# Layer 0 of a hybrid decoder: attention scores by pairs of heads, another column order in the finest decay level, query copies on GpSimd

## The chip, the cores and the metric

The kernel runs on one core of one Trainium2 chip. Its time is the device time of one execution in microseconds (us). A core has TensorE (PE in the profile, its weight loads PEld), VectorE (DVE), ScalarE (ACT), GpSimd (POOL) and SyncE (SP, which here issues every DMA). Each engine works through a queue of its own in order, and semaphores tie the queues together.

## The reference

The input is 256 tokens of width 1024. Layer 0 norms them, multiplies by one wide input matrix, and runs two mixers side by side: softmax attention (8 heads of width 64, causal, and with 256 tokens a single block, so that no block is chosen) and gated linear attention (GLA, 8 heads, keys 32 wide, values 64 wide), whose decay differs by token and key channel:

```python
b = jnp.cumsum(gi, axis=2)
diff = b[:, :, :, None, :] - b[:, :, None, :, :]
decay = jnp.exp(jnp.where(causal[:, :, None], diff, -jnp.inf))
attn = jnp.einsum('bhtd,bhsd,bhtsd->bhts', qi, ki, decay)
o = (jnp.einsum('bhts,bhsv->bhtv', attn, vi)
     + jnp.einsum('bhtd,bhdv->bhtv', qi * jnp.exp(b), state))
```

Both outputs are joined, projected back and added to the tokens. Then follow a gated convolutional feed-forward net (up to 2 x 3072, down from 3072), layer 1 (a recurrent block whose decay needs softplus(-lambda), a constant per channel), a second feed-forward net and a last norm. All of it is float32.

## The kernel before, in words

**Weights.** The large weights are cut into 204 chunks of 128 x 1024 floats (`w`). `load_w()` hands them out in order; `issue_w()` starts a chunk's DMA on SP, has ACT round it to `wh` (line 134) and DVE take the rest `wl = w - wh` (line 135). Every large product is three fast passes, `wh` with both parts of the activations and `wl` with the high part (`passes`, line 146): 24 matmuls of 256 columns for each chunk. The tiles that these products fill name the stages: `psbq`, `psbk` (GLA's q, k), `psa` (the attention's q, k), `pst` (both values), `psog` (output gate), `psout` (output projection), `psu` and `psd` (feed-forward up and down).

**Order.** The program is written in data-flow order; a scheduler places every instruction in its engine's queue and chooses memory. Only `order(a, b)` and the hooks bind it: `norm.rstd(hook=n)` makes the rounding of chunk n on ACT stand behind the norm's square root, that chunk's subtraction on DVE behind the reciprocal, and chunk n+1's rounding behind the copy of the result `rs`. Here n is 4.

**The start of layer 0.** `psg` gives the gate's low-rank product, `nps` the sum of squares and, transposed, the inverse root `rs`; `psz`, `z`, `az`, `G`, three scans (`cum`) and exponentials (`E`, `KR`) give the decays at widths 64, 16 and 4. `qn` is GLA's scaled query. `q0` is four copies of it, one for each head of a group of four, at the partitions of that head (32 rows each) with zeros elsewhere; ACT makes them (line 393), eight copies of 32 x 256. DVE multiplies `q0` by `E` into `qb`.

**GLA's scores** (`gla_attn`). Blocks of tokens are split into four levels. Levels 0 to 2 use `qb` and write runs of 64, 16 or 4 columns. The finest level uses `q0` itself: its product for offset I takes column I of every four, for the queries that it reads and for the PSUM that it writes (`pl<-q,kb`). There are 16 such products, each four heads x 32 columns. `copy_predicated` then moves what the masks `mu` allow into `at`.

**Softmax attention** (`softmax`). Head by head: scores of the first 128 queries, then the causal mask added by a bf16 product of the identity with `caus`, scores of the other 128 queries against 256 keys, mask again; DVE takes the maximum, ACT the exponentials, DVE scales, PE transposes (`ptr`) and multiplies with the values (`pso`). Even heads lie at partitions 0 to 63, odd heads at 64 to 127. Two banks (`pss`) serve in turn.

**Constants.** 23 tiny DVE instructions on 128 x 8 (lines 371 to 382, tiles `s`) make layer 1's constant `cc`; the casts of masks and identity (`mu`, `caus`, `identb`) are DVE's too. A bank is 2 KB per partition of PSUM.

Of the kernel before, what the change touches and what calls it, by code (L numbers as in the profile page):

```python
# [22 lines left out]
P = 128  # L23
S = 256
# [38 lines left out]
def trunk(ctx: ExitStack, tc: tile.TileContext, xT, w, wgk, wgk2, vec, cst, mskf, out):  # L63
# [22 lines left out]
    def V(name, i):  # L86
        o = VOFF[name] + i
        return vt[:, o:o + 1]
# [119 lines left out]
        return hi  # L208

    def residual(ps, m, X, gname, gi, norm):  # L210
        nc.vector.tensor_add(h[:, m, :], h[:, m, :], ps)  # L211
        norm.add(h[:, m, :])
        if X is not None:
            scaled_split(X, m, h[:, m, :], V(gname, gi * KT + m))

    def out_proj(M):
        acc = [bank(f"psout{i}", "g" if i < 3 else "l") for i in range(4)]
# [60 lines left out]
    with tc.tile_pool(name="l0", bufs=1) as lp, tc.tile_pool(name="l0r", bufs=4) as lr:  # L278
# [17 lines left out]
        mu = lp.tile([P, 3 * P], U8, name="mu")  # L296
        for i, n in enumerate(MSK):
            msk[n] = mu[:, i * P:(i + 1) * P]
        caus = lp.tile([P, P], BF16, name="causb")
        identb = lp.tile([P, P], BF16, name="identb")  # L300

        LV = [(1, 64, 1), (4, 16, 1), (16, 4, 1), (64, 1, 0)]
# [10 lines left out]
        q0 = [lp.tile([P, 4, S], F32, name=f"q0_{i}") for i in range(2)]  # L313
        for hf in range(2):
            nc.gpsimd.memset(q0[hf], 0.0)
        qns = {}
        at0 = [lp.tile([P, 4, S], F32, name=f"at0_{i}") for i in range(2)]
        at1 = [lp.tile([P, 4, P], F32, name=f"at1_{i}") for i in range(2)]
# [10 lines left out]
                             skip_group_check=True)  # L329
        for _ in range(4):  # L330
            nc.tensor.matmul(pw, wz[:, 0:P], wz, start=True, stop=True)
        rs = norm.rstd(hook=4)
        rtok = norm.tok
        bgk = lp.tile([32, S], F32, name="bgk")
        nc.vector.tensor_mul(bgk, psg[0:32, :S], rs[0:32, :])
        nc.sync.dma_start(ct, cst[:, P:])
        nc.sync.dma_start(mf, mskf)
        nc.vector.tensor_copy(mu, mf)
        nc.vector.tensor_copy(caus, C("caus"))
        nc.vector.tensor_copy(identb, idt)  # L340
# [30 lines left out]
        nc.vector.tensor_scalar(d2, e, 2.0, None, op0=ALU.add)
        nc.vector.reciprocal(d2, d2)
        nc.vector.tensor_mul(zz, e, d2)
        nc.vector.tensor_mul(z2, zz, zz)
        nc.vector.tensor_scalar(acc, z2, 1.0 / 17, 1.0 / 15, op0=ALU.mult, op1=ALU.add)
        for n in (13, 11, 9, 7, 5, 3, 1):
            nc.vector.tensor_mul(acc, acc, z2)
            nc.vector.tensor_scalar(acc, acc, 1.0 / n, None, op0=ALU.add)
        nc.vector.tensor_mul(acc, acc, zz)
        nc.vector.tensor_scalar(d2, lam, -1.0, 0.0, op0=ALU.mult, op1=ALU.max)  # L380
        nc.vector.scalar_tensor_tensor(acc, acc, 2.0, d2, op0=ALU.mult, op1=ALU.add)
        nc.vector.tensor_scalar(cc, acc, -8.0, None, op0=ALU.mult)
# [5 lines left out]
        for hf in range(2):  # L388
            qn = qns[hf] = lp.tile([P, S], F32, name=f"qn{hf}")
            nc.vector.scalar_tensor_tensor(qn, ps[:, hf * S:(hf + 1) * S], 32 ** -0.5, rs, op0=ALU.mult, op1=ALU.mult)  # L390
            for g in range(4):
                r = slice(32 * g, 32 * g + 32)
                nc.scalar.activation(q0[hf][r, g, :], qn[r, :], AF.Copy)
# [18 lines left out]
        def gla_prep(hf):  # L412
            hs = slice(hf * S, (hf + 1) * S)
            for li, (npar, wdt, i0) in enumerate(LV):
                def v4(ap):
                    return ap.rearrange("p (a j b) -> p a j b", j=4, b=wdt)
                kv, rv, ev = v4(kn[:, hs]), v4(KR[wdt][:, hs]), v4(E[wdt][:, hs])
                for I in range(i0, 4):
                    kb = v4(Kb[li, I])
                    J = I - i0  # L420
                    if i0:
                        nc.vector.tensor_mul(kb[:, :, J, :], kv[:, :, J, :], rv[:, :, J, :])
                    else:
# [12 lines left out]
            for li, wdt in enumerate((64, 16, 4)):  # L436
                Qb.append(lr.tile([P, 4, S], F32, tag="qb", bufs=4, name="qb"))
                nc.vector.tensor_mul(Qb[li], q0[hf], E[wdt][:, None, hs].to_broadcast([P, 4, S]))
            return Qb + [q0[hf]]

        def gla_attn(hf, qs):
            pa, pb = bank("pa", "l"), bank("pb", "l")
# [10 lines left out]
            for i in range(2):  # L453
                ts_ = slice(i * P, (i + 1) * P)
                dst = a0[:, :, 0:P] if i == 0 else a1
                for li, mn in ((1, "m64"), (2, "m16"), (3, "m4")):
                    npar, wdt, i0 = LV[li]
                    ps = bank("pl", "l")
                    def v5(ap):
                        return ap.rearrange("p g (a c) -> p g a c", c=4 * wdt)  # L460
                    pv = v5(ps.rearrange("p (g t) -> p g t", g=4))
                    qv = v5(qs[li][:, :, ts_])
                    for I in range(i0, 4):
                        cs = slice(I * wdt, (I + 1) * wdt)
                        nc.tensor.matmul(pv[:, :, :, cs], Kb[li, I][:, ts_], qv[:, :, :, cs], start=True, stop=True)  # L465
# [39 lines left out]

        PT = {}

        def softmax(hd):
            m, r = hd // 2, slice(64 * (hd % 2), 64 * (hd % 2) + 64)
            q, k = rot["q", m // 2][:, m % 2, :], rot["k", m // 2][:, m % 2, :]  # L510
            ps = bank("pss", "s")
            nc.tensor.matmul(ps[:, 0:128], q[r, 0:P], k[r, 0:P], start=True, stop=False)
            nc.tensor.matmul(ps[:, 0:128], identb, caus, start=False, stop=True)
            nc.tensor.matmul(ps[:, 128:384], q[r, P:S], k[r, 0:S], start=True, stop=False)  # L514
            nc.tensor.matmul(ps[:, 256:384], identb, caus, start=False, stop=True)
            mx = lr.tile([P, 2], F32, tag="mx", name="mx")
            nc.vector.tensor_reduce(mx[:, 0:1], ps[:, 0:128], axis=mybir.AxisListType.X, op=ALU.max)
            nc.vector.tensor_reduce(mx[:, 1:2], ps[:, 128:384], axis=mybir.AxisListType.X, op=ALU.max)
# [15 lines left out]
        av = lp.tile([P, 2, 512], F32, tag="v", name="av")  # L534
        tok_gemm(av)
        for pr in range(4):
            for j in range(2):
                PT[2 * pr + j] = softmax(2 * pr + j)
            ps = bank("pso", "t")
            for j in range(2):  # L540
                hd = 2 * pr + j
                r = slice(64 * j, 64 * j + 64)
                cs = slice(64 * hd, 64 * hd + 64)
                nc.tensor.matmul(ps[r, 0:S], av[:, 0, cs], PT[hd][:, 0:S], start=True, stop=False)
                nc.tensor.matmul(ps[r, P:S], av[:, 1, cs], PT[hd][:, S:384], start=False, stop=True)
            split(M[:, pr, 0, :], M[:, pr, 1, :], ps[:, :S])
# [53 lines left out]
        for n in range(4):  # L600
            tail(n, fin)

    def ffn(layer, X, norm, nextg):
        rs = norm.rstd()
        with tc.tile_pool(name=f"f{layer}", bufs=1) as yp, tc.tile_pool(name=f"f{layer}r", bufs=3) as fr:
# [225 lines left out]
```

## Time and profile before

| | |
|---|---|
| three timed runs | 645.31, 649.29, 649.80 us; median 649.29 |
| the profiled execution | 646.74 us; its span, first to last instruction, 645.0 us |
| busy time in the span | PE 630.7, DVE 513.3, ACT 406.0, POOL 8.9 us |
| TensorE's granted clock | 0.993 on the mean |
| read from memory | 109.01 MB, 171 GB/s |

A profile row gives the line, the engine, the operation, output and input tiles, the shape, how often, and then busy time and mean duration, or in a timeline start and length. Matmuls overlap, so a row's length holds the pipeline's depth too: what a group of matmuls costs is the distance from its start to the start of what follows.

### The profile page before, as it was taken

Reading aid. Unit: us, or ns where it says so; the run is one execution under the profiler, and the core shown is the slowest. Engines: PE = TensorE matmul, PEld = TensorE weight load, DVE = VectorE, ACT = ScalarE, POOL = GpSimd, SP = SyncE. Lnnn points to the kernel's source line nnn. Section 1 sums busy time; section 2 is a strip of 40 time slices with the busy share of each in tenths; the row PEclk is TensorE's granted clock in tenths of the full one; section 3 lists DMA queues with packets and bytes.
Section 4 is the critical chain, followed back from the end, with each engine's and each line's share of the span. In section 5 each row is a group of like instructions: output and inputs, shape, how many; then the busy total and the mean of one; then the engine's idle time right before and its main releaser. Section 6 shows DMA issues by size and latency. Waiting matters only on the chain.

```text
span 645.0 us, 12988 instructions
## 1 busy us (share of the span) xinstructions
PE 630.7 (98%) x5218; PEld 613.1 (95%) x5218; DVE 513.3 (80%) x902; ACT 406.0 (63%) x662; POOL 8.9 (1%) x36
## 2 busy tenths in 40 slices
PE   7999999999999999999999999989999999999995
PEld 4998888899999999999999999989999999999995
DVE  6699985467999999996577859996999999986532
ACT  7798454646776666675476578966666667674310
POOL 5000000000000000000000000000000000000000
PEclk8999999999999999999999999999999999999998
DMA  8823511534264485555277505544466545455201
GB/s 303 312 100 131 196 67 66 197 132 164 74 239 173 184 313 194 195 177 183 102 282 269 201 2 196 196 154 151 155 229 229 196 163 193 179 210 204 99 1 66
DMA packets 31516, 110.90 MB, mean 172 GB/s; under 512 B 3648, under 2 KB 4192, under 8 KB 31456
## 3 DMA queue, kind: packets, MB, share of 16 engines
q1 hardware_dynamic: 31456, 110.07, 47.5%
q8 instruction: 41, 0.67, 0.4%
q14 instruction: 19, 0.16, 0.1%
HBM read 109.01 MB, written 1.05 MB: 171 GB/s over the span
## 4 chain that ended last, share of the span: by engine, by line
PE 93%; DVE 2%; ACT 2%; issue 1%; DMA 1%; SPq 0%; DVEq 0%; ACTq 0%
PE psu L146 42%; PE psd L146 21%; PE psout L146 5%; PE psx L146 4%; PE psa L146 4%; PE pst L146 3%; PE psgb L146 3%; PE pl L465 2%; PE psog L146 2%; PE psgt L146 2%; PE psbq L146 1%; DVE wl L135 1%; PE psbk L146 1%; PE pss L514 1%; DMA big<-xT 1%
## 5 line engine op out<-in xcount | busy, mean ns | idle before, releaser
L134 ACT ACTIVATE wh<-w 128x1024 fp32r<-128x1024 f32 x204 | 212.5, 1056 | 112.8 <-PE psu L146 71.8
L135 DVE TENSOR_TENSOR wl<-w,wh 128x1024 fp32r<-128x1024 f32 x204 | 246.9, 1219 | 39.6 <-ACT wh L134 38.7
L146 PE MATMUL psu<-x,wh 128*128 128x256 f32 x1536 | 270.5, 280 | 0.0
L146 PEld LDWEIGHTS psu<-x,wh 128*128 128x128 f32 x1536 | 234.6, 189 | 0.0
L146 PE MATMUL psu<-x,wl 128*128 128x256 f32 x768 | 214.3, 280 | 0.0
L146 PEld LDWEIGHTS psu<-x,wl 128*128 128x128 f32 x768 | 144.7, 189 | 0.0
L146 PE MATMUL psd<-y,wh 128*128 128x256 f32 x768 | 134.6, 280 | 0.0
L146 PEld LDWEIGHTS psd<-y,wh 128*128 128x128 f32 x768 | 116.9, 188 | 0.0
L146 PE MATMUL psd<-y,wl 128*128 128x256 f32 x384 | 106.7, 279 | 0.0
L619 DVE SCALAR_TENSOR_TENSOR c<-v,big,c 128x255 f32<-128x255 f32 (+1 forms) x192 | 83.6, 475 | 0.0
L146 PEld LDWEIGHTS psd<-y,wl 128*128 128x128 f32 x384 | 72.1, 188 | 0.0
L617 ACT ACTIVATE c<-v,big 128x256 f32<-128x256 f32 x96 | 51.7, 589 | 0.6 <-DVE v L612 0.6
L172 ACT ACTIVATE sq<-big 128x256 f32<-128x256 f32 x40 | 15.4, 407 | 50.7 <-DVE big L211 50.6
L211 DVE TENSOR_TENSOR big<-big,psd 128x256 f32<-128x256 f32 x16 | 6.7, 420 | 35.3 <-PE psd L146 35.3
L612 DVE TENSOR_TENSOR v<-psu,rs 128x512 f32<-128x512 f32 x48 | 32.5, 681 | 0.0
L146 PE MATMUL psout<-r,wh 128*128 128x256 f32 x128 | 23.1, 282 | 2.0 <-DVE r L702 2.0
L146 PE MATMUL pst<-wh,x 128*128 128x256 f32 x128 | 24.2, 285 | 0.0
L146 PE MATMUL psout<-m,wh 128*128 128x256 f32 x128 | 23.7, 285 | 0.0
L146 PE MATMUL psx<-x,wh 128*128 128x256 f32 x128 | 23.0, 281 | 0.0
L146 PE MATMUL psgb<-x,wh 128*128 128x256 f32 x128 | 22.7, 280 | 0.0
L146 PE MATMUL psa<-x,wh 128*128 128x256 f32 x128 | 22.5, 280 | 0.0
L99 ACT ACT_TABLE_LOAD x17 | 21.8, 1283 | 1.0 <-PEq L823 0.7
(202 smaller groups left out, 850.5 us busy)
## 6 DMA issues: line engine op xcount, KB each, us to landing
w<-w SPq DMA_DIRECT2D x204, 512.0 KB, 4.3
big<-xT SPq DMA_DIRECT2D x4, 256.0 KB, 3.8
out<-o SPq DMA_DIRECT2D x4, 256.0 KB, 2.4
ct<-cst SPq DMA_DIRECT2D x1, 384.0 KB, 8.0
big<-vec SPq DMA_DIRECT2D x1, 224.0 KB, 7.9
mf<-mskf SPq DMA_DIRECT2D x1, 192.0 KB, 8.0
wg<-wgk SPq DMA_DIRECT2D x1, 64.0 KB, 2.0
big<-cst SPq DMA_DIRECT2D x1, 64.0 KB, 5.2
```

The lines of the kernel that those rows point to most:

```text
L99: ld = nc.scalar.preload_act_table_set(name)
L134: hi = nc.scalar.activation(wh, wt, AF.Copy)
L135: lo = nc.vector.tensor_sub(wl, wt, wh.bitcast(F32))
L146: out.append(nc.tensor.matmul(ps, a, b, start=first and i + j == 0, stop=last and i == n - 1 and j == 2, skip_group_check=skip))
L172: ins = nc.scalar.activation(sq, t, AF.Square)
L211: nc.vector.tensor_add(h[:, m, :], h[:, m, :], ps)
L465: nc.tensor.matmul(pv[:, :, :, cs], Kb[li, I][:, ts_], qv[:, :, :, cs], start=True, stop=True)
L514: nc.tensor.matmul(ps[:, 128:384], q[r, P:S], k[r, 0:S], start=True, stop=False)
L612: nc.vector.tensor_mul(v, ps.rearrange("p (j t) -> p j t", j=2), rs[:, None, :].to_broadcast([P, 2, S]))
L617: nc.scalar.activation(c[:, j, :], v[:, j, :], AF.Identity, bias=V("fc_b", layer * 48 + ch), scale=wv(2))
L619: nc.vector.scalar_tensor_tensor(c[:, j, d:], v[:, j, 0:S - d], wv(2 - d), c[:, j, d:], op0=ALU.mult, op1=ALU.add)
```

## The change

- `scores(m)` takes two heads at once, in two banks. The causal mask goes in first, one product of 256 columns for each head (`caus` now lies twice side by side), then the scores of 128 columns of both heads, then those of 256 columns of both heads. The order of these six is fixed.
- The finest GLA level writes PSUM by offset, head and column, so that every product writes 128 columns in a row. For that it reads `q1`, a copy of the query in which the columns of one offset lie together. `copy_predicated` reads PSUM through the permuted view.
- `q0` and the new `q1` (16 copies of 32 x 256 in all) are made by POOL, and the casts of `mu`, `caus` and `identb` too. Two more memsets of 128 x 1024 clear `q1`.
- The hook of the first norm is 6 instead of 4.
- The 23 DVE instructions on the tiles `s` move into `decay_const`, issued behind the first residual add of layer 0's down projection; ACT's two (`e`) stay.
- On SP the DMAs of the constants change places among themselves (`vec` first, then identity, `ct`, `gk`, `mf`); the chunks' own order stays.

```diff
-        caus = lp.tile([P, P], BF16, name="causb")
+        caus = lp.tile([P, 2, P], BF16, name="causb")
...
+        q1 = [lp.tile([P, 4, 4, S // 4], F32, name=f"q1_{i}") for i in range(2)]
+        for hf in range(2):
+            nc.gpsimd.memset(q1[hf], 0.0)
...
-        rs = norm.rstd(hook=4)
+        rs = norm.rstd(hook=6)
...
-        nc.vector.tensor_copy(mu, mf)
-        nc.vector.tensor_copy(caus, C("caus"))
-        nc.vector.tensor_copy(identb, idt)
+        nc.gpsimd.tensor_copy(mu, mf)
+        for j in range(2):
+            nc.gpsimd.tensor_copy(caus[:, j, :], C("caus"))
+        nc.gpsimd.tensor_copy(identb, idt)
...
-                nc.scalar.activation(q0[hf][r, g, :], qn[r, :], AF.Copy)
+                nc.gpsimd.tensor_copy(q0[hf][r, g, :], qn[r, :])
+            for g in range(4):
+                r = slice(32 * g, 32 * g + 32)
+                nc.gpsimd.tensor_copy(q1[hf][r, :, g, :], qn[r, :].rearrange("p (a i) -> p i a", i=4))
...
-            return Qb + [q0[hf]]
+            return Qb + [q1[hf]]
...
+                    else:
+                        pi = ps.rearrange("p (i g a) -> p i g a", i=4, g=4)
+                        for I in range(4):
+                            nc.tensor.matmul(pi[:, I], Kb[li, I][:, ts_], qs[li][:, I, :, i * 32:i * 32 + 32],
+                                             start=True, stop=True)
+                        pv = pi.rearrange("p i g a -> p g a i")
...
-            nc.tensor.matmul(ps[:, 0:128], q[r, 0:P], k[r, 0:P], start=True, stop=False)
-            nc.tensor.matmul(ps[:, 0:128], identb, caus, start=False, stop=True)
-            nc.tensor.matmul(ps[:, 128:384], q[r, P:S], k[r, 0:S], start=True, stop=False)
-            nc.tensor.matmul(ps[:, 256:384], identb, caus, start=False, stop=True)
+            both = [bank("pss", "s") for _ in range(2)]
+            seq = [nc.tensor.matmul(ps.rearrange("p (a b) -> p a b", b=P)[:, 0:3:2, :], identb, caus, start=True, stop=False,
+                                    skip_group_check=True) for ps in both]
+            for tq, cs in ((0, slice(0, 128)), (1, slice(128, 384))):
+                for j, ps in enumerate(both):
+                    r = slice(64 * j, 64 * j + 64)
+                    seq.append(nc.tensor.matmul(ps[:, cs], q[r, tq * P:(tq + 1) * P], k[r, 0:(tq + 1) * P], start=False,
+                                                stop=True, skip_group_check=True))
...
-                residual(ps[:, :S], m, Xn, nextg[0] if nextg else None, nextg[1] if nextg else 0, nn)
+                add = residual(ps[:, :S], m, Xn, nextg[0] if nextg else None, nextg[1] if nextg else 0, nn)
+                if nextg and m == 0:
+                    decay_const(add)
...
+    def decay_const(after):
+        o = nc.vector.tensor_scalar(d2, e, 2.0, None, op0=ALU.add)
+        order(after, o)
...
```

Three places show what this makes of the queues. The first is ACT's queue around the first norm's square root, `rtk<-nps`; `wh<-w` is a chunk's rounding, `z<-psz` the way on to the decays. Before:

```order
L369 ACTIVATE s_286<-big 128x8
L108 ACTIVATE rtk<-nps,big 128x2
L99 ACT_TABLE_LOAD
L108 ACTIVATE s_286<-s_286 128x8
L134 ACTIVATE wh_412<-w_410 128x1024
L198 ACTIVATE rs<-nps 128x256
L134 ACTIVATE wh_455<-w_453 128x1024
L134 ACTIVATE wh_485<-w_483 128x1024
L134 ACTIVATE wh_525<-w_523 128x1024
L393 ACTIVATE q_0_212<-qn_366 32x256 x4
L393 ACTIVATE q_1_213<-qn_372 32x256 x4
L347 ACTIVATE z<-psz,big 128x256 x2
```

And now:

```order
L134 ACTIVATE wh_402<-w_400 128x1024
L134 ACTIVATE wh_445<-w_443 128x1024
L108 ACTIVATE rtk<-nps,big 128x2
L99 ACT_TABLE_LOAD
L108 ACTIVATE s_291<-s_291 128x8
L134 ACTIVATE wh_475<-w_473 128x1024
L198 ACTIVATE rs<-nps 128x256
L134 ACTIVATE wh_515<-w_513 128x1024
L134 ACTIVATE wh_545<-w_543 128x1024
L134 ACTIVATE wh_585<-w_583 128x1024
L352 ACTIVATE z<-psz,big 128x256 x2
L353 ACTIVATE az<-z 128x512
```

Two roundings (chunks 4 and 5) have moved ahead of the root, one less stands between the root and `rs`'s users, and the query copies are gone from in front of `z`.

The second place is PE's queue at the first two heads' scores (`rotq`, `rotk` are their rotated queries and keys, `identb` and `causb` the mask product, `pst` a large product). Before:

```order
L512 MATMUL pss<-rotk_658,rotq_518 128x128
L513 LDWEIGHTS identb
L513 MATMUL pss<-causb,identb 128x128
L514 MATMUL pss<-rotk_658,rotq_518 128x256
L515 LDWEIGHTS identb
L515 MATMUL pss<-causb,identb 128x128
L512 MATMUL pss<-rotk_658,rotq_518 128x128
L513 LDWEIGHTS identb
L513 MATMUL pss<-causb,identb 128x128
L514 MATMUL pss<-rotk_658,rotq_518 128x256
L515 LDWEIGHTS identb
L515 MATMUL pss<-causb,identb 128x128
```

Now the first pair's two masks stand far ahead of its scores, between the last `psbk` product and `psz`; they wait for POOL's cast of `causb`:

```order
L146 MATMUL psbk<-x,wl_373 128x256
L514 LDWEIGHTS identb
L514 MATMUL pss<-causb,identb 128x2x128
L514 LDWEIGHTS identb
L514 MATMUL pss<-causb,identb 128x2x128
L348 MATMUL psz<-bgk,gk_168 128x256 x2
L146 MATMUL psa<-x,wh_402 128x256 x2
```

and the scores themselves stand together, some 200 rows later:

```order
L146 MATMUL pst<-wl_796,x 128x256
L146 MATMUL pst<-wh_795,x 128x256
L519 MATMUL pss<-rotk_648,rotq_508 128x128 x2
L519 MATMUL pss<-rotk_648,rotq_508 128x256 x2
L462 MATMUL pl<-qb,kb_3_196 128x8x16
L146 MATMUL pst<-wh_795,x 128x256
```

Eight products in a row, four of them of the full height, have become four of half height there, and two of full height elsewhere. The masks of the other pairs stand only a few rows ahead of their scores, and in the second pair one group of `ptr` transpositions stands between the two kinds of score.

The third place is DVE's queue behind the norm's reciprocal (`rtk<-rtk`), where `s` are the tiny constants and `wl<-w,wh` a chunk's subtraction. It reads before:

```order
L191 RECIPROCAL rtk<-rtk 128x2
L371 TENSOR_SCALAR s_287<-s_286 128x8
L372 RECIPROCAL s_287<-s_287 128x8
L373 TENSOR_TENSOR s_288<-s_286,s_287 128x8
L374 TENSOR_TENSOR s_289<-s_288 128x8
L380 TENSOR_SCALAR s_287<-big 128x8
L135 TENSOR_TENSOR wl_413<-w_410,wh_412 128x1024
L375 TENSOR_SCALAR s_290<-s_289 128x8
L335 TENSOR_TENSOR bgk<-psg,rs 32x256
L390 SCALAR_TENSOR_TENSOR qn_366<-psbq,rs 128x256
L390 SCALAR_TENSOR_TENSOR qn_372<-psbq,rs 128x256
L401 TENSOR_TENSOR ct<-ct,rs 128x256
```

And now:

```order
L135 TENSOR_TENSOR wl_403<-w_400,wh_402 128x1024
L135 TENSOR_TENSOR wl_446<-w_443,wh_445 128x1024
L191 RECIPROCAL rtk<-rtk 128x2
L135 TENSOR_TENSOR wl_476<-w_473,wh_475 128x1024
L339 TENSOR_TENSOR bgk<-psg,rs 32x256
L383 SCALAR_TENSOR_TENSOR qn_348<-psbq,rs 128x256
L383 SCALAR_TENSOR_TENSOR qn_358<-psbq,rs 128x256
L397 TENSOR_TENSOR ct<-ct,rs 128x256
L398 TENSOR_TENSOR ct<-ct,rs 128x256
L135 TENSOR_TENSOR wl_516<-w_513,wh_515 128x1024
L135 TENSOR_TENSOR wl_546<-w_543,wh_545 128x1024
```

The tiles `s` are gone from here, and the subtractions of chunks 4 and 5 stand ahead of the reciprocal instead of behind it.

More of the change, by code (lines that the diff above doesn't have):

```diff
@@ L210, in residual @@
     def residual(ps, m, X, gname, gi, norm):
-        nc.vector.tensor_add(h[:, m, :], h[:, m, :], ps)
+        add = nc.vector.tensor_add(h[:, m, :], h[:, m, :], ps)
         norm.add(h[:, m, :])
@@ L214, in residual @@
             scaled_split(X, m, h[:, m, :], V(gname, gi * KT + m))
+        return add
     def out_proj(M):
@@ L370, in trunk @@
         act(LNEXP, e, e, AF.Exp, scale=-1.0)
[L371 to L382, printed above, removed]
         ps = bank("psbq")
@@ L460, in v5 @@
                         return ap.rearrange("p g (a c) -> p g a c", c=4 * wdt)
[L461 to L465, printed above, removed]
+                    if wdt > 1:
+                        pv = v5(ps.rearrange("p (g t) -> p g t", g=4))
+                        qv = v5(qs[li][:, :, ts_])
+                        for I in range(i0, 4):
+                            cs = slice(I * wdt, (I + 1) * wdt)
+                            nc.tensor.matmul(pv[:, :, :, cs], Kb[li, I][:, ts_], qv[:, :, :, cs], start=True, stop=True)
+                    else:
[4 more added lines that the diff above has]
+                        pv = pi.rearrange("p i g a -> p g a i")
                     c0 = i0 * wdt
@@ L506, in trunk, with scores, softmax @@
         PT = {}
-        def softmax(hd):
-            m, r = hd // 2, slice(64 * (hd % 2), 64 * (hd % 2) + 64)
+        def scores(m):
             q, k = rot["q", m // 2][:, m % 2, :], rot["k", m // 2][:, m % 2, :]
[L511 to L515, printed above, removed]
+            both = [bank("pss", "s") for _ in range(2)]
[6 more added lines that the diff above has]
+                                                stop=True, skip_group_check=True))
+            for a_, b_ in zip(seq, seq[1:]):
+                order(a_, b_)
+            return both
+        def softmax(ps):
             mx = lr.tile([P, 2], F32, tag="mx", name="mx")
@@ L536, in trunk @@
         for pr in range(4):
-            for j in range(2):
-                PT[2 * pr + j] = softmax(2 * pr + j)
+            for j, ps in enumerate(scores(pr)):
+                PT[2 * pr + j] = softmax(ps)
             ps = bank("pso", "t")
@@ L601, in trunk @@
             tail(n, fin)
+    def decay_const(after):
+        o = nc.vector.tensor_scalar(d2, e, 2.0, None, op0=ALU.add)
+        order(after, o)
+        nc.vector.reciprocal(d2, d2)
+        nc.vector.tensor_mul(zz, e, d2)
+        nc.vector.tensor_mul(z2, zz, zz)
+        nc.vector.tensor_scalar(acc, z2, 1.0 / 17, 1.0 / 15, op0=ALU.mult, op1=ALU.add)
+        for n in (13, 11, 9, 7, 5, 3, 1):
+            nc.vector.tensor_mul(acc, acc, z2)
+            nc.vector.tensor_scalar(acc, acc, 1.0 / n, None, op0=ALU.add)
+        nc.vector.tensor_mul(acc, acc, zz)
+        nc.vector.tensor_scalar(d2, lam, -1.0, 0.0, op0=ALU.mult, op1=ALU.max)
+        nc.vector.scalar_tensor_tensor(acc, acc, 2.0, d2, op0=ALU.mult, op1=ALU.add)
+        nc.vector.tensor_scalar(cc, acc, -8.0, None, op0=ALU.mult)
     def ffn(layer, X, norm, nextg):
```

## The prediction, made before the changed kernel was run

> **What bounds the kernel now.** I read the page first (busy time, the chain that ended last), then stages of layer 0 in the view by windows, then PE's timeline there.
>
> ```profile
> span 645.0 us, 12988 instructions
> PE 630.7 (98%) x5218; PEld 613.1 (95%) x5218; DVE 513.3 (80%) x902; ACT 406.0 (63%) x662; POOL 8.9 (1%) x36
> PE 93%; DVE 2%; ACT 2%; issue 1%; DMA 1%; SPq 0%; DVEq 0%; ACTq 0%
> 25.00:57.00 32.00, 31.00 (x259) 30.35 (x257) 30.10 (x49) 31.56 (x53) 0.00 (x0) 1.00 0.38 133
> 57.00:63.00 6.00, 5.63 (x44) 5.53 (x45) 6.00 (x18) 3.16 (x5) 0.00 (x0) 1.00 0.70 260
> 63.00:122.70 59.70, 59.70 (x418) 49.67 (x418) 40.13 (x107) 29.75 (x76) 0.00 (x0) 1.00 0.37 133
> ```
>
> In the window rows the columns behind the stretch are PE, PEld, DVE, ACT and POOL. PE makes 93% of the chain, so a microsecond taken from PE's queue is one off the span, unless something else is late there. From 63 to 122.7 us, where all scores lie, PE is busy throughout at full clock (1.00), and DVE (40.13 of 59.70) and ACT (29.75) have room. From 25 to 57 us ACT (31.56 of 32.00) and DVE (30.10) are full, and PE falls behind them once:
>
> ```profile
> 50.96 4.62 DVE L438 TENSOR_TENSOR qb<-q,E 128x1024 f32<-128x1024 f32 x4
> ...
> 56.10 1.21 DVE L135 TENSOR_TENSOR wl<-w,wh 128x1024 fp32r<-128x1024 f32 x1
> ...
> 55.24 0.40 PE L146 MATMUL pst<-wh,x 128*128 128x256 f32 x2
> 55.48 0.28 PE L146 MATMUL pst<-wl,x 128*128 128x256 f32 x1
> 55.60 0.40 PE L146 MATMUL pst<-wh,x 128*128 128x256 f32 x2
> 57.37 0.39 PE L146 MATMUL pst<-wl,x 128*128 128x256 f32 x1 [1.37 <-DVE wl L135]
> ```
>
> Two such products cost 0.24 us from start to start (55.24 to 55.48), so PE loses 57.37 - 55.60 - 0.24 = **1.5 us** to a subtraction that stands behind four `qb`.
>
> **Part 1, the finest level.** Same shape, other columns:
>
> ```profile
> L465 PE MATMUL pl<-q,kb 128*128 128x128 f32 x32 | 8.2, 407 | 0.0
> L465 PE MATMUL pl<-qb,kb 128*128 128x128 f32 x48 | 7.4, 277 | 0.0
> ...
> 89.40 1.99 PE L465 MATMUL pl<-q,kb 128*128 128x128 f32 x8
> 91.03 0.59 PE L146 MATMUL psog<-x,wh 128*128 128x256 f32 x2
> ...
> 104.40 1.99 PE L465 MATMUL pl<-q,kb 128*128 128x128 f32 x8
> 106.31 0.66 PE L544 MATMUL pso<-PT,av 128*64 128x256 f32 x4
> ...
> 109.54 0.83 PE L465 MATMUL pl<-qb,kb 128*128 128x128 f32 x6
> 110.13 0.37 PE L146 MATMUL psog<-x,wl 128*128 128x256 f32 x1
> ...
> 110.66 1.99 PE L465 MATMUL pl<-q,kb 128*128 128x128 f32 x8
> 112.57 0.66 PE L562 MATMUL pob<-at,bv 128*64 128x256 f32 x4
> ```
>
> A float32 matmul leaves two records. Four products of the finest level take 1.63, 1.91 and 1.91 us to the next start, on the mean 1.82; four such groups (x32) 7.3. Three of a coarser level, with columns in runs, take 0.59, so one 0.197 and sixteen 3.1. The new form writes and reads runs of 32 or more. **Gain 4.1 us.** Bounds: nothing, if what costs is something else than the stride, and 4.1.
>
> **Part 2, the scores.** A pair of heads now, and a pair of half-width products that lie in different halves of the array:
>
> ```profile
> 63.64 0.49 PE L512 MATMUL pss<-rotk,rotq 64*128 64x128 f32 x2
> 64.05 0.23 PE L513 MATMUL pss<-causb,identb 128*128 128x128 bf16 x1
> 64.21 0.70 PE L514 MATMUL pss<-rotk,rotq 64*128 64x256 f32 x2
> 64.84 0.23 PE L515 MATMUL pss<-causb,identb 128*128 128x128 bf16 x1
> 65.00 0.49 PE L512 MATMUL pss<-rotk,rotq 64*128 64x128 f32 x2
> ...
> 66.25 0.37 PE L146 MATMUL pst<-wh,x 128*128 128x256 f32 x1
> ...
> 106.80 0.39 PE L545 MATMUL pso<-PT,av 128*64 128x128 f32 x4
> 107.12 0.51 PE L146 MATMUL psog<-x,wh 128*128 128x256 f32 x2
> ```
>
> A pair costs 66.25 - 63.64 = 2.61 us: per head 0.41 and 0.63 for scores and 0.16 twice for masks. Full-height masks between half-height scores keep the two heads apart. What two heads cost when they share the array, these rows show only for columns: `pso` does 256 and 128 columns of two heads in 107.12 - 106.31 = 0.81 us, less than one head's scores now (1.04). I take 0.81 for the scores of a pair, as the nearest row of two heads at once. A mask of 256 columns is not in the trace: one of 128 takes 0.16, and a score pays 0.22 for its further 128 columns in two records, the mask's single record half of that, so 0.27. A pair: 0.81 + 2 x 0.27 = 1.35, gain 1.26, four times 5.0. One pair is cut by transpositions between its two kinds of score; I charge 0.2 for it. **Gain 4.8 us.** Bounds: heads that follow each other give 2 x 1.04 + 2 x 0.27 = 2.62 a pair, so no gain; with masks at no price it is 4 x 1.80 = 7.2.
>
> **Part 3, the start.** What goes from DVE and ACT ahead of the late subtraction:
>
> ```profile
> 20.21 0.26 ACT L108 ACTIVATE rtk<-nps,big 128x2 f32<-128x2 f32 x1 [4.72 <-PE nps L187]
> 26.41 3.39 ACT L393 ACTIVATE q<-qn 32x256 f32<-32x256 f32 x8
> ...
> 20.51 0.17 DVE L191 RECIPROCAL rtk<-rtk 128x2 f32<-128x2 f32 x1 [3.23 <-ACT rtk L108]
> L378 DVE TENSOR_SCALAR s<-s 128x8 f32<-128x8 f32 x7 | 1.2, 169 | 0.2
> ```
>
> DVE loses 23 tiny instructions of about 0.17 us (3.9 us) and three casts, and it does chunks 4 and 5 in the 3.23 us in which it now waits for the root. At 1.21 each (the row of the 56.10 subtraction) that is 2.4 us more. ACT does their rounding in its 4.72 idle us and drops 3.39 us of copies, so `z`, the scans and `qb` come earlier. About 6.3 us on DVE against a lateness of 1.5: **gain 1.5 us**, and no more, since PE is then fed. Bounds: 1.5, or minus 1.5 if POOL hinders DVE as below. Of the moved root: if chunk 5 landed later than the sum of squares is done, the root would wait for it; I see ACT idle 4.72 us before the root, and two roundings take 2.1.
>
> **At nothing.** The tiny instructions go where DVE waits 14.3 us for ACT within the 65 us of the down projection:
>
> ```profile
> L135 DVE TENSOR_TENSOR wl<-w,wh 128x1024 fp32r<-128x1024 f32 x29 | 35.1, 1223 | 14.3 <-ACT wh L134 14.3
> ```
>
> 3.9 us fit there; without that cover a residual add would come up to 0.2 us late behind one of them. The two early masks wait for POOL's cast and delay `psz` by their own 0.54, already counted. `copy_predicated` through the permuted view may get slower; DVE has 19 us of room in that stage. The casts and memsets on POOL run before 25 us, when it does nothing.
>
> **POOL's copies** are priced nowhere in the trace: POOL does only memsets.
>
> ```profile
> 8.73 0.31 POOL L321 MEMSET at<- 128x256 f32 x1
> ```
>
> The nearest rows are this memset with the same 256 elements per partition (0.31) and ACT's copy of the same tile (3.39 / 8 = 0.42). I take 0.42, 16 times 6.7 us from about 25.8 us, when `qn` is there (bounds 0.31 and, as the far end, several times ACT's). The fourth `qb` needs twelve of them. Before, `qb` ran from 50.96; some 6 us earlier its fourth starts at about 48.4. So a copy may take (48.4 - 25.8) / 12 = 1.9 us before DVE waits. [...]
>
> **The sum.** 4.1 + 4.8 + 1.5 = 10.4 us. The profiled execution took 646.74 (its span 645.0): 646.74 - 10.4 = **636.3 us**. That execution lies inside the three runs (645.31 to 649.80) and 2.55 below their median, 649.29; from the median it would be 638.9. I keep 636.3, the execution whose rows the terms come from.
>
> **Rivals.**
> - *Heads that do not overlap.* Masks no longer break the row, but scores of two heads follow each other, nothing instead of 4.8: 641.1. For it: no row shows two halves by rows at once. Against: `pso` does it by columns, and the banks differ.
> - *POOL hinders DVE.* If POOL's reads and DVE's instructions with two inputs in SBUF (`wl`, `G`, the scans) exclude each other, 16 copies of 0.42 hold DVE up by 6.7 us, all of the 6.3 that it gained, and PE keeps its wait of 1.5, or 0.4 more: 637.8 to 638.2. No row shows POOL reading beside DVE, for or against. [...]
> - *Softmax turns into the wait.* The masks of the next pair need the banks that exponentials still read. Between the third pair's scores and the fourth's first mask stand 23 large products (0.117 each, half of 0.24), 6 coarse and 2 finest (0.197) and two groups of three transpositions (110.66 - 110.33 = 0.33 each), together 4.9 us; the chain is four maxima and one head's exponentials:
>
> ```profile
> L518 DVE TENSOR_REDUCE mx<-pss 128x1 f32<-128x256 f32 x8 | 3.3, 410 | 0.0
> L517 DVE TENSOR_REDUCE mx<-pss 128x1 f32<-128x128 f32 x8 | 2.3, 285 | 4.2 <-PE pss L515 4.1
> 110.33 0.49 PE L529 MATMUL ptr<-big,pe 128*128 128x128 f32 x3
> 72.33 0.37 ACT L108 ACTIVATE pe<-pss,mx 128x128 f32<-128x128 f32 x1 [0.66 <-DVE mx L519]
> ```
>
>   at most 2 x 0.70 plus about 0.9, so 2.3 us, and one subtraction (1.21) ahead still fits. If DVE's queue were 4 us late there and at the two other pairs, each would give back 1.5: 640.8.
> - *Slower: POOL far slower than ACT.* At 1.9 us a copy DVE begins to wait with `qb`, and PE, fed from behind it, waits with it. To eat the whole gain, twelve copies must end 10.4 us later still: 2.8 us each, nine times the memset. At 4 us each they end 48 - 22.6 = 25.4 us late: 661.7.
> - *It does not do what it says*, if the stride was not what cost 0.455 a product (1.82 / 4): 640.4. Against it: nothing else differs between the two `pl` rows.
>
> **How the numbers follow.** Forecast 0.52; heads in a row 0.15; POOL and DVE 0.13; softmax waits 0.10; stride not the cause 0.05; POOL slow 0.05. A measurement of this kernel tells about 1% from no change, 6.5 us: faster is below 642.8 by the median. Every case but the slow POOL lies below that; with the runs' own spread (4.5 us) I give faster 0.83, same 0.12, slower 0.05. The range takes in the rivals up to heads in a row and most of the spread's half below (4.3 us under the forecast): 632 to 642.5.
>
> **What will show it.** In the changed profile: four `pl<-q` products in about 0.8 us; a pair's scores in about 0.8 with the second head's first record before the first head is done; no PE wait for `wl` near 56 us; ACT's `z` well before the end of the old copies (26.41 + 3.39 = 29.8 us); POOL's copies between 26 and 35 us; PE's `psout` starting about 10 us earlier than 122.7 us, where the window above ends; and the stages from 180 us on unchanged. I am wrong if PE shows idle time for `pss`, `ptr` or `qb` in layer 0, if a pair still takes 2.5 us, or if POOL's copies run past 48 us.

## The result, and the profile after

The changed kernel takes **637.49 us** (median of 4 runs, 637.13 to 639.27) against 647.42 for the kernel before (4 runs, 645.31 to 649.80); the ratio is 0.9848, with a 95% interval of 0.9815 to 0.9881. Measured again later it was 638.77 against 648.12, ratio 0.9863 (0.9839 to 0.9887). One execution each of experiments 8 and 9 below took 875.77 and 3470.93 us, far outside all others, and is left out of their figures. Otherwise the runs of either kernel differ among themselves with the mean clock that TensorE was granted, so like must be compared with like:

```
mean granted clock   before (all runs)    changed (all runs)
0.996 to 0.997       645.0 to 646.1       637.1 to 637.7
0.991 to 0.995       646.7 to 648.8       638.7 to 639.3
0.987 to 0.989       648.9 to 650.4       none
```

At equal clock the gain is about 8 us, and between the two profiled executions (0.993 and 0.992) it is 646.74 - 639.27 = **7.5 us**, where 10.4 were forecast. Both of these have one stretch at half clock near the start, behind a PE that was busy for 1.96 of 3 us before and 2.41 of 3 us in the changed kernel (8 to 11 us): the granted clock was 0.50 from 12 to 15 us before, 0.75 and 0.68 in the two slices of 3 us from 12 us on in the changed one. The page of the changed kernel (span, busy time, chain by engine):

```profile
span 637.5 us, 12979 instructions
PE 622.5 (98%) x5210; PEld 608.1 (95%) x5210; DVE 516.8 (81%) x899; ACT 402.5 (63%) x654; POOL 33.3 (5%) x58
PE 92%; DVE 3%; ACT 2%; issue 1%; DMA 1%; SPq 0%; DVEq 0%
```

Two of the prediction's stretches in the view by windows (columns PE, PEld, DVE, ACT, POOL, granted clock); the last one ends where `psout` starts now:

```profile
25.00:57.00 32.00, 30.24 (x249) 29.32 (x248) 31.03 (x41) 26.24 (x42) 19.13 (x16) 1.00 0.30 102
63.00:115.20 52.20, 52.20 (x425) 46.17 (x423) 38.74 (x101) 28.72 (x74) 0.00 (x0) 1.00 0.41 144
```

PE is still the bound. The stretch with the scores is 7.5 us shorter and full. But between 25 and 57 us PE is busy for 30.24 us, less than before (31.00): it lost its wait for `wl` and found a longer one. PE's timeline of the changed kernel (start, length, then the instruction):

```profile
25.96 0.39 PE L514 MATMUL pss<-causb,identb 128*128 128x256 bf16 x2
26.28 1.13 PE L348 MATMUL psz<-bgk,gk 32*128 32x256 f32 x4
...
40.56 0.48 PE L146 MATMUL psa<-x,wh 128*128 128x256 f32 x2 [1.76 <-DVE kn L394]
...
66.38 0.93 PE L519 MATMUL pss<-rotk,rotq 64*128 64x128 f32 x8
67.23 0.49 PE L462 MATMUL pl<-qb,kb 128*128 128x128 f32 x2
...
74.99 1.05 PE L466 MATMUL pl<-q,kb 128*128 128x128 f32 x8
75.88 0.39 PE L462 MATMUL pl<-qb,kb 128*128 128x128 f32 x2
```

All four scores of a pair take 67.23 - 66.38 = 0.85 us, two masks 0.32 (26.28 - 25.96), four products of the finest level 0.89 (75.88 - 74.99). At 38.8 us the third tile `psa` needs the PSUM bank of `psbk`, which `kn` frees, and `kn` stands on VectorE behind the scans. PE waits 1.76 us for it, its only wait above 0.15 us between 24 us and the first `psu`; before, that was the one for `wl`. VectorE's timeline there:

```profile
31.42 1.44 DVE L135 TENSOR_TENSOR wl<-w,wh 128x1024 fp32r<-128x1024 f32 x1 [0.34 <-ACT wh L134]
32.79 1.13 DVE L357 SCALAR_TENSOR_TENSOR G<-z,az 128x512 f32<-128x512 f32 x1
34.02 4.52 DVE L362 TENSOR_TENSOR_SCAN cum<-cum,G 128x512 f32<-128x512 f32 x3
...
39.74 0.68 DVE L394 TENSOR_TENSOR kn<-psbk,rs 128x512 f32<-128x512 f32 x1
40.34 2.58 DVE L403 TENSOR_TENSOR KR<-cum 128x512 f32<-128x512 f32 x3
...
44.04 5.51 DVE L434 TENSOR_TENSOR qb<-q,E 128x1024 f32<-128x1024 f32 x4
```

In the kernel before, the same groups read:

```profile
38.27 0.68 DVE L352 SCALAR_TENSOR_TENSOR G<-z,az 128x512 f32<-128x512 f32 x1
...
40.60 3.45 DVE L357 TENSOR_TENSOR_SCAN cum<-cum,G 128x512 f32<-128x512 f32 x3
...
47.42 0.68 DVE L398 TENSOR_TENSOR kn<-psbk,rs 128x512 f32<-128x512 f32 x1
48.02 1.88 DVE L407 TENSOR_TENSOR KR<-cum 128x512 f32<-128x512 f32 x3
```

`G`, the scans, the `KR` group and the `qb` (shown in the prediction) took 0.68, 3.45, 1.88 and 4.62 us; here they take 1.13, 4.52, 2.58 and 5.51. Beside them GpSimd copies (its timeline; single copies and one group of four):

```profile
26.41 0.46 POOL L386 COPY q<-qn 32x256 f32<-32x256 f32 x1 [8.23 <-DVE qn L383]
27.44 3.90 POOL L386 COPY q<-qn 32x256 f32<-32x256 f32 x1
31.39 0.40 POOL L386 COPY q<-qn 32x256 f32<-32x256 f32 x1
...
41.37 4.82 POOL L389 COPY q<-qn 32x256 f32<-32x256 f32 x4
```

One copy takes 0.46 us, the next but one 3.90: it lies behind three subtractions that VectorE does in one go from 27.60 to 31.08. A copy in VectorE's gap at 31.39 takes 0.40. The sixteen end at 46.19 us and take 19.6 us in all. Last, ScalarE's `z`, in the changed kernel and then in the one before:

```profile
28.23 0.82 ACT L352 ACTIVATE z<-psz,big 128x256 f32<-128x256 f32 x2
```

```profile
29.82 0.84 ACT L347 ACTIVATE z<-psz,big 128x256 f32<-128x256 f32 x2
```

`z` comes 1.6 us earlier than before. In this execution ScalarE had to wait 0.51 us for the second load of the input (at 6.96 us), which did not happen in the profiled execution before.

To see where 7.5 us come from, I added up on PE's timeline, for each tile, the time from each record to the start of the next, up to the first `psu` (148.13 us before, 140.68 after):

```
                              before   after   difference
first psbq product starts     10.40    11.39    +0.99   loads of the input
psa and pst (with the waits)  48.12    48.58    +0.46   wait 1.37 became 1.76
pss                           10.31     4.91    -5.40
pl                            12.33     8.06    -4.27
pa, pb, pob, psog             19.47    20.53    +1.06   no run takes this apart
everything else                                 -0.29
sum                                             -7.45   (140.68 - 148.13)
```

### The profile page after: what moved, and what is told of

Same layout as the page of the kernel before. It is cut to its first block, busy times and chain, and to the rows that moved or that the text cites. A ratio compares the mean times of both kernels' runs of the same rounds, so it can differ in the third digit from the quotient of the medians.

```text
span 637.5 us, 12979 instructions
## 1 busy us (share of the span) xinstructions
PE 622.5 (98%) x5210; PEld 608.1 (95%) x5210; DVE 516.8 (81%) x899; ACT 402.5 (63%) x654; POOL 33.3 (5%) x58
## 4 chain that ended last, share of the span: by engine, by line
PE 92%; DVE 3%; ACT 2%; issue 1%; DMA 1%; SPq 0%; DVEq 0%
PE psu L146 42%; PE psd L146 21%; PE psout L146 5%; PE pst L146 4%; PE psx L146 4%; PE psgb L146 3%; PE psa L146 2%; PE psog L146 2%; PE psgt L146 2%; DVE wl L135 1%; PE psbq L146 1%; PE pl L462 1%; PE psbk L146 1%; ACT wh L134 1%; DMA big<-xT 1%
```

## The experiments

All are the changed kernel but for the edit shown. Times are compared with 637.1 to 637.7 us at a clock of 0.997 and 638.7 to 639.3 at 0.992 to 0.994.

**1. What the step of four elements costs: reading.** The finest level writes in runs as now, but reads `q0` with the old step; `q1` is gone.

```
-  matmul(pi[:, I], Kb[li, I][:, ts_], qs[li][:, I, :, i*32:i*32+32])
+  matmul(pi[:, I], Kb[li, I][:, ts_], qv[:, :, :, I])      # qv: view of q0, step 4
-  gpsimd.tensor_copy(q1[hf][r, :, g, :], ...)              # 8 copies
```

> The finest level writes its products in runs of 32 again as the changed kernel does, but reads q0 with a step of four elements, as the kernel before did; q1 and its eight copies on GpSimd are left out. Theory A (the write into PSUM with a step is what cost 0.24 us a product): four products stay at about 0.9 us, and the time is that of the changed kernel, 637.5 us, or up to 1.8 us less because GpSimd copies half as much (wait for kn 1.76 us in the changed kernel): 635.7 to 637.5. Theory B (the read with a step is what cost): four products take 1.82 us again, four groups give back 3.8 us: 639.5 to 641.3. If both share the cost, four products lie between, near 1.35 us.

**2. And writing.** It reads `q1` in runs, and writes PSUM with the old step.

```
-  matmul(pi[:, I], ...)
+  matmul(pv[:, :, :, I], ...)                              # step 4 in PSUM
```

> The finest level reads q1 in runs of 32, but writes with a step of four elements as the kernel before did; all else is the changed kernel, all sixteen copies too. Theory A (write): four products take 1.82 us again, 3.8 us more in all, 641.3 us. Theory B (read): four products stay at about 0.9 us, 637.5 us. If the step is not the cause at all, neither this run nor the one with a strided read changes the products.

Measured: 641.15 to 641.43 us (clock 0.993) with the strided read, 637.26 to 639.48 (0.992 to 0.997) with the strided write. The groups of the finest level, by line and form (busy time, mean of one), in the first and in the second run:

```profile
L461 PE MATMUL pl<-q,kb 128*128 128x128 f32 x32 | 8.1, 404 | 0.0
```

```profile
L466 PE MATMUL pl<-q,kb 128*128 128x128 f32 x32 | 4.3, 275 | 0.0
```

The strided read brings back the old mean (404 ns; 407 before), the strided write leaves the new one (275). Theory B holds: **the read was the whole cost**, and rearranging the PSUM side gained nothing. The sum over `pl` is 3.3 us longer with the strided read; the time is 1.9 to 2.7 us longer at equal clock, because with half the copies PE's wait for `kn` is 0.6 us instead of 1.8.

**3. Scores head by head again.**

```
-  both = [bank("pss") ...]; masks of both; 128 of j=0, 128 of j=1, 256 of j=0, 256 of j=1
+  per head: scores 128, mask, scores 256, mask             # as in the kernel before
```

> Scores head by head with each mask behind its score, as in the kernel before; all else is the changed kernel. Theory (two heads share the array when their products alternate; the changed kernel's rows show 0.86 us for the scores of a pair and 0.32 for its masks, together 1.18, against 2.61 before): 4 x 1.43 = 5.7 us more, 643.2 us. With the forecast's terms (1.35 a pair, 0.2 for the cut) it would be 4.8 more, 642.3. Rival (the two heads do not overlap, and the drop came from the earlier place of the masks): little change, 637.5 to 638.5.

Measured: 643.88 us median of 10 (642.49 to 642.96 at 0.995 to 0.996, 643.76 to 644.60 at 0.993, one 646.47 at 0.991). That is 4.5 to 5.9 us more at equal clock, and the sum over `pss` is 10.20 instead of 4.91. PE's waits at the start are others here (1.1 us for `kb` and 0.6 for ScalarE's copies of `pa`, in place of 1.76 for `kn`), but together as long. The groups of the 256-column scores, of this run and then of the changed kernel:

```profile
L517 PE MATMUL pss<-rotk,rotq 64*128 64x256 f32 x16 | 5.6, 428 | 0.0
```

```profile
L519 PE MATMUL pss<-rotk,rotq 64*128 64x256 f32 x16 | 2.5, 390 | 0.0
```

A record is hardly shorter (390 against 428 ns), but the sixteen together keep PE busy for 2.5 us instead of 5.6: records of two heads lie over each other. The theory holds; whether it takes the alternation this run cannot tell, since it also puts the masks between the scores.

**4. Must the two heads alternate?**

```
-  for tq in (0, 1):  for j in (0, 1): score(tq, j)
+  for j in (0, 1):   for tq in (0, 1): score(tq, j)
```

> The four score products of a pair stand head by head (128 and 256 columns of one head, then of the other) instead of alternating; masks stay ahead of them. Theory A (products overlap only with a neighbour of the other head): one of three borders is mixed, 1.04 + 1.04 - 0.4 = 1.7 us a pair instead of 0.86, 3.3 us more in four pairs: 640.8 us. Theory B (no overlap at all, the drop was the masks): no change, 637.5, and the pair at 0.86 again. Theory C (overlap needs strict alternation, a single border gives nothing): 2.08 a pair, 4.9 more, 642.4 us.

Measured: 639.47 us (638.50 to 638.56 at 0.996, 640.39 to 640.52 at 0.994), 0.8 to 1.8 more at equal clock. PE's timeline of a pair that stands together and of the one that transpositions cut in two:

```profile
65.87 0.93 PE L519 MATMUL pss<-rotk,rotq 64*128 64x128 f32 x8
66.73 0.49 PE L462 MATMUL pl<-qb,kb 128*128 128x128 f32 x2
...
76.59 0.92 PE L519 MATMUL pss<-rotk,rotq 64*128 64x128 f32 x4
77.44 0.55 PE L539 MATMUL ptr<-big,pe 128*128 128x128 f32 x3
77.92 0.92 PE L519 MATMUL pss<-rotk,rotq 64*128 64x128 f32 x4
78.77 0.50 PE L146 MATMUL pst<-wh,x 128*128 128x256 f32 x2
```

None of the three theories gave this. Both heads in a row take 0.86 us, as they do alternating, and **one head alone takes 0.85**. So the second head is free as long as it is a neighbour, in either order; the cut pair pays for both, 1.70 instead of 0.42 + 0.63. The sum over `pss` is 0.68 us longer (5.59); the rest of the time lies in products that stand elsewhere in the new order.

**5. Do the copies on GpSimd slow VectorE?** All sixteen are left out, so the decayed branch computes on zeros.

> All sixteen copies on GpSimd are left out, so q0 and q1 keep their zeros and the decayed branch computes on zeros; every other instruction stands where it stood. Theory (GpSimd's copies slow the instructions of VectorE beside them): G goes from 1.13 back to 0.68 us, the three scans from 4.52 to 3.45, the KR group from 2.58 to 1.88, the four qb from 5.51 to 4.62, and PE's wait for kn (1.76 us) falls to at most 0.2: 635.8 us. Rival (something else, DMA or ScalarE, stretches VectorE there): these rows stay, the wait stays, 637.5 us.

Measured: 636.74 us (636.33 to 637.25 at 0.993 to 0.994), 1.4 to 3.0 us less at equal clock. VectorE's timeline, and the window row from 25 to 60 us:

```profile
32.52 0.69 DVE L357 SCALAR_TENSOR_TENSOR G<-z,az 128x512 f32<-128x512 f32 x1
33.32 3.46 DVE L362 TENSOR_TENSOR_SCAN cum<-cum,G 128x512 f32<-128x512 f32 x3
...
38.41 1.89 DVE L397 TENSOR_TENSOR KR<-cum 128x512 f32<-128x512 f32 x3
...
41.41 4.63 DVE L428 TENSOR_TENSOR qb<-q,E 128x1024 f32<-128x1024 f32 x4
```

```profile
25.00:60.00 35.00, 35.00 (x287) 34.11 (x287) 33.71 (x56) 31.36 (x50) 0.00 (x0) 1.00 0.40 137
```

Every stretched group is back at its old length, and PE is busy 35.00 of 35.00 us. The theory holds.

**6. What a copy costs by itself.** Sixteen more copies of both forms on a scratch tile, in the down projection of layer 0 (one run).

```
+  gpsimd.tensor_copy(xd[r, g, :], xs[r, :])                # x8, in runs
+  gpsimd.tensor_copy(xd[...step layout...], xs[r, :].rearrange("p (a i) -> p i a", i=4))   # x8
```

> Sixteen more copies of the same two forms on GpSimd, from a scratch tile into a scratch tile, in the down projection of layer 0, where VectorE has idle time between its subtractions; the results are unused. Theory A (a copy is slow by itself on GpSimd): 1.2 us and more each, alone too. Theory B (VectorE beside it makes it slow): copies in VectorE's idle time take 0.3 to 0.6 us, those beside its subtractions 1.2. The time stays at 637.5 in both, since PE waits for nothing there.

Measured: 638.48 us (clock 0.992), unchanged. GpSimd's timeline (a copy in runs that starts ahead of a subtraction, one that starts behind one, one with the step that nothing holds up), and VectorE's beside the first two:

```profile
292.17 0.39 POOL L634 COPY xd<-xs 32x256 f32<-32x256 f32 x1
...
300.64 1.36 POOL L634 COPY xd<-xs 32x256 f32<-32x256 f32 x1
...
302.51 0.66 POOL L637 COPY xd<-xs 32x256 f32<-32x256 f32 x1
```

```profile
292.19 1.46 DVE L135 TENSOR_TENSOR wl<-w,wh 128x1024 fp32r<-128x1024 f32 x1
...
300.52 1.21 DVE L135 TENSOR_TENSOR wl<-w,wh 128x1024 fp32r<-128x1024 f32 x1
301.66 0.37 DVE L625 TENSOR_SCALAR s<-s 128x8 f32<-128x8 f32 x1
```

Theory B holds. A copy that is not held up takes 0.39 us, with the step 0.66. The subtraction that starts just behind such a copy (292.19) takes 1.46 instead of 1.21. The copy that starts at 300.64, while VectorE subtracts from 300.52 to 301.73, ends at 302.00, behind all of the subtraction. The small instruction that follows, with one input (`s<-s`), takes 0.37 instead of 0.17 and ends at 302.03, behind the copy. So in these rows the two engines take turns, whole instruction by whole instruction. In the changed kernel `kn`, one of whose two inputs lies in PSUM, takes 0.68 us as before although a copy starts inside it, and that copy (40.11 us) takes its 0.39.

**7. `kn` ahead of the scans.** The block with `G`, scans and `E` is written behind `kn`, and `G` is ordered after it.

```
   kn_op = vector.tensor_mul(kn, psbk, rs)
+  g_op = vector.scalar_tensor_tensor(G, z, 0.0, az, ...); order(kn_op, g_op); scans, E
```

> kn stands on VectorE ahead of G and the three scans instead of behind them; the copies on GpSimd stay. Theory A (PE's 1.76 us are the place of kn behind scans that GpSimd stretches): the wait for kn goes; what stands behind it on VectorE is as long as before, and PE then comes to the first product that reads kb about 1.7 us earlier, at about 50.1 us, while kb is done at about 50.9, so 0.5 to 0.8 us come back there: 636.2 to 636.5 us. Theory B (nothing comes back): 635.7. Rival (VectorE's whole queue is what PE waits for, so the wait only moves to kb): 637.5.

Measured: 636.54 us (635.09 to 635.34 at 0.996, 637.74 to 637.95 at 0.989 to 0.992), 0.7 to 2.6 us less at about equal clock. PE's timeline:

```profile
48.84 0.70 PE L442 MATMUL pa<-qb,kb 128*128 128x256 f32 x2 [0.83 <-DVE kb L419]
```

Theory A holds: the wait for `kn` is gone, and 0.83 us come back at the first product that reads `kb`.

**8. `q0` back on ScalarE**, ahead of `z`; `q1` stays on GpSimd.

```
-  gpsimd.tensor_copy(q0[hf][r, g, :], qn[r, :])
+  scalar.activation(q0[hf][r, g, :], qn[r, :], Copy)
```

> The eight copies to q0 back on ScalarE, ahead of z as in the kernel before; the eight to q1 stay on GpSimd. z then comes about 3.4 us later, the scans and qb with it, and kn goes behind the first qb as in the kernel before, with no PE product waiting for its bank. Theory (VectorE's relief of the small instructions is enough by itself): no PE wait in this stretch, 635.7 us. Rival (the later z makes VectorE late again, as in the kernel before): PE waits 1.4 us for wl or up to 2 us for kb near 50 to 56 us: 637.2 to 637.8.

Measured: 644.75 us (median of 9; 642.98 to 646.32 at 0.986 to 0.990). Both expectations were far off. Timelines of ScalarE and PE, and the window row behind PE's pause, in which 0.51 is the granted clock:

```profile
31.02 0.84 ACT L352 ACTIVATE z<-psz,big 128x256 f32<-128x256 f32 x2
```

```profile
48.04 0.77 PE L146 MATMUL psa<-x,wh 128*128 128x256 f32 x2 [4.25 <-DVE kn L394]
```

```profile
48.00:54.00 6.00, 5.96 (x28) 5.99 (x29) 6.00 (x10) 5.95 (x12) 0.00 (x0) 0.51 0.00 0
```

`z` comes 2.8 us later than in the changed kernel (31.02 against 28.23), everything that hangs on it goes back, and `kn` with it, to 47.21. I had expected that no product would wait for its bank; the fourth tile `psa` did, 4.25 us. And after that pause TensorE was granted half its clock (0.51) until 54 us: by my estimate, six microseconds at half speed are another 3 lost.

**9. `kn` first, and `q1` on ScalarE** behind the exponentials of `KR`.

> kn ahead of G, and the eight copies to q1 on ScalarE behind the exponentials of KR, so that GpSimd does only the eight copies to q0, from about 26 to 36 us. If the stretching of VectorE is GpSimd's, the KR group and the qb are back at 1.88 and 4.62 us and the scans at about 3.8; PE waits for neither kn nor kb: 635.7 us, as without any copy. If ScalarE's eight copies (0.42 to 0.6 us each, 3.4 to 4.8 in all, in a stretch where it waits 3.35 us) come to stand ahead of something that PE needs, up to 1.5 us come back: 637.2.

Measured: 640.20 us (median of 3; 639.85 to 640.27 at 0.992 to 0.994), 0.6 to 1.6 us slower than the changed kernel at equal clock, and worse than the rival gave. Timelines of ScalarE and PE:

```profile
44.81 4.75 ACT L435 ACTIVATE q<-qn 32x256 f32<-32x256 f32 x7
```

```profile
59.09 0.71 PE L463 MATMUL pl<-qb,kb 128*128 128x128 f32 x4 [2.23 <-ACT at L448]
```

VectorE is free again, but the copies (0.68 us each) push roundings and the copies of `pa` back, and PE waits 2.23 us for a bank that these hold.

**10. The same copies later**, behind ScalarE's copy of `pb` (the first at 64.23 us instead of 44.81).

```
   at_op = scalar.activation(a0[:, :, 128:256], pbv, Copy)
+  order(at_op, scalar.activation(q1[hf][r, :, g, :], qns[hf]..., Copy))     # 8 copies
```

> kn ahead of G as in the run with kn first, and the eight copies to q1 on ScalarE, but only behind its copies of pb, from about 58 us, where ScalarE is half idle and q1 is needed 15 us later; GpSimd does the eight copies to q0 alone. Theory: KR and qb are back at 1.88 and 4.62 us, kb is in time, and PE waits for neither kn, kb nor the copies of pa: 2.5 to 3 us less than the changed kernel in the same call (PE's 1.76 us, and the 0.3 to 0.8 that each copy off GpSimd gives back), 634.5 to 635 us against 637.5. Rival (ScalarE's 5.4 us of copies delay av and the exponentials there): PE waits for those instead, and the time is that of kn first, 636.5, or more.

Measured: **635.29 us** (median of 6; 634.58 to 635.30 at 0.996 to 0.997, 636.01 to 636.13 at 0.994), ratio to the kernel before 0.9813 (0.9790 to 0.9837). The changed kernel once more, measured beside it:

> The changed kernel once more, as the measure for the other runs of this call: 637.5 us, with PE's wait of 1.8 us for kn and twelve of the sixteen copies on GpSimd at 1.2 to 1.4 us.

It took 638.77 us (637.06 at 0.997, 638.66 to 639.27 at 0.992 to 0.994), so the new version is 1.8 to 2.8 us faster at equal clock. Its window row:

```profile
25.00:60.00 35.00, 35.00 (x290) 34.24 (x289) 34.90 (x57) 30.25 (x49) 9.75 (x8) 1.00 0.43 137
```

PE is busy throughout this stretch, and the theory holds: the three `KR` take 0.67 to 0.68 us each again. One wait is new behind it, 0.58 us at 119.48 us for ScalarE's last copy `PT`, of the kind that the rival named. This is the fastest version of the study.

**11. The small constants at the start again.**

```
-  decay_const(add) in the down projection
+  the same 23 instructions behind the exponential of lam, as before
```

> The 23 small instructions of the layer-1 constants stand at the start again, as before the change; all else is the changed kernel. Theory (VectorE's queue ahead of kn is what PE waits for): six of them stand between bgk and kn outside VectorE's idle time, 0.1 to 0.2 us each, and the rest lies in idle time or behind kn, ahead of the qb and kb: PE's wait grows from 1.76 to 2.1 to 2.8 us, with up to 1 us more at kb: 638 to 639.5 us. Rival (VectorE's idle time of 2.31 and 0.84 us takes them all): 637.5.

Measured: 639.69 us (639.13 to 639.33 at 0.994), at that clock 0.3 to 0.7 us more than the changed kernel measured beside it; 640.05 at 0.992 and 641.27 at 0.989. As a difference that is the lower end of what the theory gave, but not by its way: PE's wait for the bank did not grow (1.8 us); a wait of 0.7 us for ScalarE's copies of `pa` came later. VectorE's timeline shows why:

```profile
33.32 0.37 DVE L383 TENSOR_SCALAR s<-s 128x8 f32<-128x8 f32 x1
33.60 0.68 DVE L357 SCALAR_TENSOR_TENSOR G<-z,az 128x512 f32<-128x512 f32 x1
34.20 0.61 DVE L382 TENSOR_TENSOR s<-s,s 128x8 f32<-128x8 f32 x1
```

The small instructions take over the waiting for GpSimd (0.37 and 0.61 instead of 0.17), and `G` behind one is back at 0.68. The turn is paid once, by whoever stands there; so moving them away from the start was worth only some 0.5 us, not the 3.9 of their own time.

## Why the prediction was right, and where it was not

The forecast was 636.3 us, 1.2 below the measured median; the gain of 10.4 us was too large by 2.9 for the profiled executions. That the median lies so close is in part luck: three of the four runs had a mean clock of 0.997, where the execution that the forecast starts from had 0.993, and the changed kernel took 639.27 at 0.992. By its steps:

- **Part 1, the finest level, 4.1 us: right**, 7.42 to 3.33 us over the rows of the finest level. The stride was the cause (runs 1 and 2), and the trace of before could not tell that it was the read alone.
- **Part 2, the scores, 4.8 us: right in mechanism, 0.6 too small.** A pair's scores take 0.85 where 0.81 was taken from `pso`; the masks 0.16 each, not 0.27: ahead of the scores, 256 columns of a mask cost no more than 128 did between them. The cut of one pair was priced at 0.2; it costs 0.32 + 0.42 + 0.63 - 1.17 = 0.20. The rival of heads that follow each other is out (runs 3 and 4), and that of softmax waits too: PE shows none for `pss` or `ptr`.
- **Part 3, the start, 1.5 us: wrong; the wait became 0.4 us longer.** VectorE got its relief and lost it again. Two steps failed. The first is the price of GpSimd's copies: 0.42 us is right for a copy in runs that is not held up (0.39 to 0.46), but beside VectorE sixteen took 19.6 us, 1.23 each, and held VectorE up by about 3.8 us in return (`G` 0.44, scans 1.06, `KR` 0.69, `qb` 0.88, two subtractions 0.36, the two `ct` 0.41). This was the rival "POOL hinders DVE", given 0.13; its mechanism came about beside the main forecast, not in its place. Its price for the wait, "1.5, or 0.4 more", fits the measured 1.76 against 1.37 only by luck: it had the copies hold VectorE up by 6.7 us and the wait stay at `wl`; they held it up by 3.8, and the wait moved. Its time, 637.8 to 638.2, even lies nearer to the measured ones than the forecast's; only the rows tell the two apart. The second is the sentence "PE is then fed": I looked for the next wait at `wl` and `qb`. In the kernel before `kn` ran at 47.42 us with no product behind it; now its bank goes to a product that is due at 38.8. I had followed VectorE's queue, not which bank each `psa` product gets.
- **The copies with a step** take 0.66 us where nothing holds them up (run 6), not the 0.42 that the forecast had for all sixteen. The break point of 1.9 us a copy was not reached on the mean (1.23).
- **At nothing: right.** The small instructions in the down projection cost nothing (7.45 us ahead at the first `psu`, 7.5 at the end); `copy_predicated` of the finest level takes 737 ns through the permuted view, 732 before.
- **Not foreseen:** 0.99 us from the loads at the start. The change does touch them: the identity's load, which stood ahead of chunks 1 to 3, now stands behind them. But in the twelve other profiled runs, whose loads stand in the new order too, the first `psbq` product starts between 10.20 and 11.56 us (11.39 here, 10.40 before), so this trace alone doesn't tell what part is the change's. Then 1.06 us in `pa`, `pb`, `pob` and `psog`, perhaps from other neighbours in the new order; that is not shown. Nor does any run take back the hook of 6 or the casts on GpSimd by themselves.

Of the signs that I named, `z` early, the pairs, the finest level, no wait for `wl` and the unchanged later stages came; the copies' end at 35 us (46.2) and `psout` 10 us earlier (7.5) did not. Of the signs of being wrong none came, since a wait for `kn` was not among them.

## What to carry to other kernels

A copy moved to an idle GpSimd was not free here: where VectorE worked back to back on inputs outside PSUM (subtractions, scans, `qb`), each took its turn behind a whole instruction of the other, so copies of 0.39 to 0.66 us took 1.23 on the mean and cost VectorE 0.24 each. After any relief of a busy engine look for the next thing that PE needs from it, PSUM banks that it frees included, and give that a place ahead in the queue. Products that use one half of the array's rows should stand next to a product of the other half, as here: the second was free in either order (0.85 and 0.86 us for four products of two heads, 0.85 for two of one head), and full-height products between them ended that (1.70 us for the cut pair of run 4).

## What the runs showed of the hardware that I had not expected

- A step of 16 bytes costs a float32 product of 128 columns on the read side (404 against 275 ns a record) and nothing on the PSUM side (275 ns).
- Half-height products of the two halves overlap without alternating: 0.86 us for four of two heads in a row, 0.85 for two of one head.
- A GpSimd copy of 0.39 us took 3.90 us behind three subtractions of VectorE without a gap: it got in only where VectorE paused. Beside the scans, without a gap too, the engines took turns one for one (copies of 1.47 and 1.48 us, scans of 1.48 to 1.60 instead of 1.15).
- An instruction of VectorE that reads one input from PSUM was not held up by a copy, nor held it up (`kn` 0.68 us, the copy 0.39).
- After a pause of PE of 4.25 us the granted clock was 0.51 for 6 us; after pauses of 1.76 and 2.23 us it stayed at 1.00.
